# A query stage in two passes by tokens, and sixteen more prompt tokens that fetch their own expert rows

## The chip, the cores and the metric

The kernel runs on one core of one Trainium2 chip. The metric is the device time of one launch in microseconds (us). The kernel before took 1719.96 us, the median of three runs (1716.91 to 1726.47). A core has five engines with a queue of instructions each, which they work off in order: TensorE (PE; its weight loads are shown as PEld), VectorE (DVE), ScalarE (ACT), GpSimd (POOL) and SyncE (SP), which here only issues DMAs. POOL also issues the gathering DMAs. [...]

## The reference, cut to what matters

One layer over 512 prompt tokens and 128 sample tokens (8 sequences of 16), width 1024. The first half is a mixer (linear recurrence and sliding-window attention), and the change doesn't touch it. The second half, which takes most of the time, is a product-key expert layer:

```python
def peer(xn, w_query, sub_keys1, sub_keys2, expert_u, expert_v):
    q = (xn @ w_query).reshape(T, 8, 2, 128)                 # 8 heads, two halves
    s1 = einsum('thd,kd->thk', q[:, :, 0], sub_keys1)        # 128 keys a half
    s2 = einsum('thd,kd->thk', q[:, :, 1], sub_keys2)
    v1, i1 = top_k(s1, 16); v2, i2 = top_k(s2, 16)
    cand_s = v1[..., :, None] + v2[..., None, :]             # 256 pairs, of which 16 stay
    top_s, top_pos = top_k(cand_s, 16)
    idx = take_along_axis(i1 * 128 + i2, top_pos)            # 16 of 16384 experts
    gates = softmax(top_s)
    act = gelu(einsum('thkd,td->thk', expert_u[idx], xn))
    return einsum('thk,thkd->td', gates * act, expert_v[idx])
y = h + peer(rmsnorm(h))
```

So each token picks, in each of 8 heads, 16 experts out of 16384, and an expert is one row of `expert_u` and one of `expert_v` (1024 floats, 4 KB each).

## The kernel before, in words

Tokens lie in five tiles of 128: tiles 0 to 3 are the prompt, tile 4 is the samples. There are two ways to the expert layer. The first 448 prompt tokens (`SD`) go the *dense* way: all 16384 experts are multiplied with all 448 tokens, and a gate matrix that is zero nearly everywhere weighs the results. The 128 sample tokens and the last 64 prompt tokens (`HD`) go the *own* way: their expert rows are fetched one by one with gathering DMAs of 128 rows (one row to a partition).

Every fp32 matmul is done as three: an operand is split into a high part (rounded, by ACT) and a low part (the rest, by a subtraction), and high*high, high*low and low*high are added up. A weight *slab* of 1 MB is loaded by SP (`raw`), `high` (L93) makes `wh` on ACT, and `low` (L98, the work stands at L100) makes `wl` on the engine that it is given, POOL or DVE. `raw`, `wh` and `wl` have two buffers each.

The stages after the mixer, in order of the program:

1. *Query stage* (L840 to L966). The normed tokens are turned to columns by `turn_rows` (`xh`, `xl`). Eight slabs of `w_query` give 16 units `u` (head and half): a unit multiplies 128 query columns with all 640 tokens (`query_half`, then `proj_T`, two matmuls of 320 columns to each of 24 steps). `query_keys(u - 2)` then multiplies the finished queries of the unit two before with the 128 keys (five small matmuls, L914), copies the scores with ACT (L916), and finds the 16 best of each token on DVE (L919 to L924). In every second unit `next_slab(G)` splits the next slab, the low part on POOL.
2. *U stage* (loop at L1285, 64 iterations `c`). Each takes a slab of `expert_u` with 256 experts: 48 matmuls of 448 columns (`u_block`, L960), a gelu on ACT (L1280), and the result goes to DRAM (`Ad`). Beside it, DVE works through the *pieces*: `select(t)` joins the two halves' best to 16 experts with gates, and `matrix(t)` builds the gate matrix from one-hot pieces (L1122, L1126), which PE multiplies (L1134). `plan` deals the pieces out over the iterations by an estimated cost (`piece(2.4, ...)` is 2.4 us), evenly up to iteration `NS - 6`.
3. *V stage* (loop at L1339, 64 iterations). Each takes a slab of `expert_v`: `weigh` multiplies the activations with the gates on DVE (L1266), `weigh_split` splits them on ACT (L1271) and DVE (L1273), and 48 matmuls of 448 columns (L1359) add up.

The own way runs beside stages 2 and 3: `own_work(c)` first consumes on DVE the rows that have come (a dot product with the token at L1181, or a weighted addition at L1186) and then lets POOL fetch the next (L1174), three or four per iteration, 384 in all (192 of `u`, 192 of `v`), into a ring of six buffers. The work starts when `select(4)` is done.

Nothing reorders the program: each engine runs its instructions in the order in which the code writes them.

## Time and profile before

| | before |
|---|---|
| median of three runs | 1719.96 us |
| the profiled execution | 1711.95 us, its span 1710.2 us |
| PE / DVE / ACT / POOL busy | 98% / 83% / 40% / 40% of the span |
| bytes moved | 492.67 MB, mean 288 GB/s |
| chain that ended last | PE 75%, DVE 14%, DMA 5%, ACT 3%, issue 2% |

The times of instructions are those of the profiled execution, counted from the start of its span. A busy PE is not a PE at its peak, since matmuls overlap: a matmul of 448 columns is shown as 366 ns long while the next starts after about 202 ns. So the pace is read from starts, or from how many stand in a stretch. [...]

### The profile page before, as it was taken

What the parts mean: (1) busy time and instruction counts of PE and PEld (TensorE: products, weight loads), DVE (VectorE), ACT (ScalarE), POOL (GpSimd) and SP (SyncE); (2) the same over time, 40 slices, a digit from 0 to 9 for tenths busy, and PEclk for the clock granted to TensorE, in tenths of its full rate; (3) what the DMA queues carried; (4) which work ended last, traced back from release to release, by engine and by line L of the source; (5) the groups of instructions that cost most, each with busy time, mean ns of one, the idle gap of its engine ahead of it and who ended that gap; (6) DMA issues with size and microseconds to landing.
All of it is one profiled execution on the core that took longest, in us unless ns stands there. A gap on an engine that the chain in (4) does not pass through costs nothing.

```text
span 1710.2 us, 24851 instructions
## 1 busy us (share of the span) xinstructions
PE 1679.2 (98%) x9654; PEld 1546.7 (90%) x9654; DVE 1417.1 (83%) x2348; ACT 679.6 (40%) x790; POOL 690.2 (40%) x485
## 2 busy tenths in 40 slices
PE   8999999999999999999999999899999999999998
PEld 8887889999989898999899999899998999999998
DVE  7766465999789999899988885788887888888886
ACT  5457332233444544554455553322232232232322
POOL 4122003233134344444444433455454555455551
PEclk9999899999999999999999999999999999999999
DMA  5313233223689898999999999999999999999995
GB/s 169 104 48 113 76 105 90 75 70 126 249 277 322 308 377 291 370 389 348 314 379 344 372 352 403 397 380 368 384 374 335 405 376 385 375 377 376 369 350 201
DMA packets 180983, 492.67 MB, mean 288 GB/s; under 512 B 16817, under 2 KB 75057, under 8 KB 170225
## 3 DMA queue, kind: packets, MB, share of 16 engines
q1 hardware_dynamic: 124848, 288.68, 46.7%
q0 software_dynamic: 55296, 201.35, 31.4%
q8 instruction: 75, 1.23, 0.3%
q10 hardware_dynamic: 720, 1.05, 0.2%
q14 instruction: 44, 0.35, 0.1%
HBM read 426.11 MB, written 65.48 MB: 287 GB/s over the span
## 4 chain that ended last, share of the span: by engine, by line
PE 75%; DVE 14%; DMA 5%; ACT 3%; issue 2%; POOL 0%; DVEq 0%; ACTq 0%; SPq 0%
PE po L1359 35%; PE pa L960 21%; PE pa L113 7%; PE pb L1134 3%; DVE wl L100 2%; DMA gt<-Gd 2%; PE pb L638 2%; PE pa L638 2%; DVE ring L1181 2%; DVE h_rows L1181 2%; DMA raw<-in_u 2%; PE pb L914 1%; PE pa L857 1%; ACT wh L95 1%; DMA Gd<-stage 1%
## 5 line engine op out<-in xcount | busy, mean ns | idle before, releaser
L1359 PE MATMUL po<-ph,wh 128*128 128x448 f32 x1024 | 374.7, 366 | 3.5 <-ACT act L1280 1.9
L1359 PE MATMUL po<-pl,wh 128*128 128x448 f32 x1024 | 374.9, 366 | 3.2 <-DVE pl L1273 3.2
L100 DVE TENSOR_TENSOR wl<-raw,wh 128x2048 fp32r<-128x2048 f32 x135 | 308.8, 2288 | 83.5 <-ACT wh L95 82.8
L960 PE MATMUL pa<-xh,wh 128*128 128x448 f32 x1024 | 377.5, 369 | 0.0
L1359 PE MATMUL po<-ph,wl 128*128 128x448 f32 x1024 | 374.5, 366 | 0.0
L960 PE MATMUL pa<-xh,wl 128*128 128x448 f32 x1024 | 374.2, 365 | 0.2 <-DVE wl L100 0.2
L960 PE MATMUL pa<-xl,wh 128*128 128x448 f32 x1024 | 374.1, 365 | 0.0
L95 ACT ACTIVATE wh<-raw 128x2048 fp32r<-128x2048 f32 x146 | 279.5, 1914 | 226.9 <-PE po L1359 173.8
L1174 POOL DMA_INDIRECT h_rows<-in_u_rows,rowi x96 | 138.5, 1443 | 219.9 <-DVE h_rows L1181 164.1
L1174 POOL DMA_INDIRECT ring<-in_u_rows,rowi x96 | 136.8, 1425 | 194.3 <-DVE ring L1181 173.4
L1174 POOL DMA_INDIRECT h_rows<-in_v,rowi x96 | 155.9, 1624 | 143.4 <-DVE h_rows L1186 121.3
L1359 PEld LDWEIGHTS po<-ph,wh 128*128 128x128 f32 x1024 | 192.7, 188 | 19.5 <-ACT act L1280 2.2
L1359 PEld LDWEIGHTS po<-pl,wh 128*128 128x128 f32 x1024 | 192.7, 188 | 19.0 <-DVE pl L1273 3.8
L960 PEld LDWEIGHTS pa<-xh,wl 128*128 128x128 f32 x1024 | 192.3, 188 | 16.1 <-DVE wl L100 0.6
L1359 PEld LDWEIGHTS po<-ph,wl 128*128 128x128 f32 x1024 | 192.7, 188 | 15.3
L960 PEld LDWEIGHTS pa<-xh,wh 128*128 128x128 f32 x1024 | 192.4, 188 | 15.2 <-ACT act L1280 0.3
L960 PEld LDWEIGHTS pa<-xl,wh 128*128 128x128 f32 x1024 | 192.5, 188 | 15.1
L1174 POOL DMA_INDIRECT ring<-in_v,rowi x96 | 149.8, 1560 | 133.2 <-DVE h_rows L1186 109.2
L1280 ACT ACTIVATE act<-pa 128x448 f32<-128x448 f32 x128 | 71.5, 559 | 232.4 <-PE pa L960 225.1
L1271 ACT ACTIVATE ph<-at 128x896 fp32r<-128x896 f32 x64 | 61.0, 953 | 254.0 <-DVE at L1266 254.0
L1142 ACT ACTIVATE stage<-pb 128x512 f32<-128x512 f32 x112 | 109.8, 1129 | 89.9 <-PE pb L1134 89.9
L1273 DVE TENSOR_TENSOR pl<-at,ph 128x896 fp32r<-128x896 f32 x64 | 69.9, 1093 | 72.7 <-ACT ph L1271 72.7
(280 smaller groups left out, 2498.7 us busy)
## 6 DMA issues: line engine op xcount, KB each, us to landing
raw<-in_u SPq DMA_DIRECT2D x64, 1024.0 KB
raw<-in_v SPq DMA_DIRECT2D x64, 1024.0 KB
Ad<-act SPq DMA_DIRECT2D x64, 448.0 KB
Gd<-stage SPq DMA_DIRECT2D x28, 1024.0 KB
gt<-Gd SPq DMA_DIRECT2D x64, 448.0 KB
at<-Ad SPq DMA_DIRECT2D x64, 448.0 KB
raw<-in_w_query SPq DMA_DIRECT2D x8, 1024.0 KB
raw<-in_w_out SPq DMA_DIRECT2D x4, 1024.0 KB
```

Source lines behind the costliest of these rows:

```text
L95: A.activation(wh, raw, AF.Copy)
L100: eng.tensor_sub(wl, raw, wh.bitcast(F32))
L113: PE.matmul(ps[:, hf, :H2], a[:, k, cs], b[:, k, hf * H2:(hf + 1) * H2], start=(k == 0 and n == 0), stop=(k == KD - 1 and n == 2))
L638: PE.matmul(ps, a[:, k0 + k, ts_], b[:, k, :], start=(k == 0 and n == 0), stop=(k == CT - 1 and n == 2))
L960: PE.matmul(u_ps[c, n][:, :SD], a[:, k, n * P:(n + 1) * P], b[:, k, :SD], start=(k == 0 and m == 0), stop=(k == KD - 1 and m == 2))
L1142: A.activation(d["stage"][:, :, t0:t0 + 4].rearrange("p j t -> p t j"), d[n, f], AF.Copy, scale=1.0 / GSC)
L1174: G.indirect_dma_start(out=rows[n], out_offset=None, in_=table, in_offset=bass.IndirectOffsetOnAxis(ap=rowi[:, c:c + 1], axis=0))
L1181: V.scalar_tensor_tensor(row, row, 1.0, xrow[:, n // NS_], op0=ALU.mult, op1=ALU.mult, accum_out=dots[:, n:n + 1])
L1271: A.activation(ph, a2, AF.Copy)
L1273: V.tensor_sub(pl, a2, ph.bitcast(F32))
L1280: A.activation(act[c][:, n], u_ps[c, n][:, :SD], AF.Gelu_apprx_tanh)
L1359: PE.matmul(po[k][:, :SD], a[:, j, k * P:(k + 1) * P], b[:, j, :], start=(c == 0 and j == 0 and n == 0), stop=(c == NS - 1 and j == 1 and ...
```

## The change

The prompt tokens on the own way become 80: the last 64 as before, and 16 more (rows 48 to 63 of tile 3, `NC`). The dense width `SD` falls from 448 to 432. For these 16 tokens the rows are laid out with one head to a group of 16 partitions, so that their 2048 rows fill 16 more fetches of 128; a fetch round is now 208 rows of `u` and 208 of `v` (`NR`). Their outputs are summed over the 8 groups through DRAM at the end (`Yc`).

The query stage is written in two passes. The first multiplies all eight slabs with the own tiles 3 and 4 (256 columns), the second loads and splits the eight slabs again and multiplies them with tiles 0 to 2 (384 columns). In the second pass DVE works on `select(4)` and on the search of the dense tiles, as far as a budget of 4.2 us to a unit goes; the searches that are left are pieces of the U stage. Fetching starts in the second pass, one row per unit. The scores of the dense tiles wait in the `stage` buffers.

```diff
-SD = S - HD
+NC = 16
+C0 = P - HD - NC
+SD = S - HD - NC
-        + [i["w_out"][n] for n in range(4)] + [i["w_query"][n] for n in range(PH)]
+        + [i["w_out"][n] for n in range(4)] + [i["w_query"][n] for _ in range(2) for n in range(PH)]
...
+    def queries(ps, w, n, cols):
+        wh, wl = w
         for k in range(KD):
             for m, (a, b) in enumerate(((wh, xh), (wh, xl), (wl, xh))):
+                PE.matmul(ps[:, :cols.stop - cols.start], a[:, k, n * P:(n + 1) * P], b[:, k, cols],
                           start=(k == 0 and m == 0), stop=(k == KD - 1 and m == 2))
...
+    turn_rows(ND - 1)
+    turn_rows(ND)
+    scaled(turns[-1])
     for n in range(2):
-        query_half(n, 1)
+        queries(two[n], kc(slabs[A0 + 2]), n, OWN)
+        turn_rows(n)
+    turn_rows(2)
...
+    next_slab(G)
+    for u in range(2):
+        query_out(u, two[u], OWN)
+    for u in range(2, 2 * PH):
+        ps = wide()[:, 0]
+        queries(ps, kc(slabs[Q0 + u // 2]), u % 2, OWN)
+        own_keys(u - 2)
+        if u % 2 == 0:
+            next_slab(G)
+        query_out(u, ps, OWN)
...
+    for u in range(2 * PH):
+        ps = wide()[:, 0]
+        queries(ps, kc(slabs[Q0 + PH + c]), n, DENSE)
+        if u < 2:
+            own_keys(2 * PH - 2 + u)
+        else:
+            scores(u - 2 + 2 * PH, 3, later(u - 2))
+        for f in acts:
+            f()
+        if n == 0:
+            if c + 1 < PH:
+                next_slab(G)
+            else:
+                put(U, 0, G)
+                u_load(1)
+        query_out(u + 2 * PH, ps, DENSE)
+        used = max(used, 0.0) - 4.2
+        while used < 0:
...
+        if not todo:
+            own_step(n_pre, n_pre + 1)
+            n_pre += 1
...
+            if c == NR - 1:
+                nc.sync.dma_start(Yc.rearrange("h (t q) d -> (h t) (q d)", t=NC), y)
+                parts = p2.tile([P, PH, P], F32, name="parts", tag="y2")
+                nc.sync.dma_start(parts, Yc.rearrange("h r d -> r h d"))
+                rest = p2.tile([P, 2, P], F32, name="rest")
+                nc.sync.dma_start(rest[:, 0], Hd[ND - 1, C0:HD].rearrange("t (q d) -> (t q) d", d=P))
+                V.tensor_reduce(rest[:, 1], parts.rearrange("p h d -> p d h"), axis=AX.X, op=ALU.add)
+                V.tensor_add(rest[:, 0], rest[:, 0], rest[:, 1])
...
+                for dst, src in ((slots, ts), (rowi, ti)):
+                    nc.sync.dma_start(dst[0:HD, NS_:NB_], src[up, :HD])
+                    for h in range(PH):
+                        nc.sync.dma_start(dst[h * NC:(h + 1) * NC, NB_:], src[C0:HD, h * TK:(h + 1) * TK])
```

ACT in the query stage, two units of before: the score copies are L916, the split of the next slab L95, the copy of the unit's queries L905.

```order
L916 ACTIVATE s<-pb 128x512
L916 ACTIVATE s<-pb 128x128
L95 ACTIVATE wh<-raw 128x2048
L905 ACTIVATE q<-pa 128x640
L916 ACTIVATE s<-pb 128x512
L916 ACTIVATE s<-pb 128x128
L905 ACTIVATE q<-pa 128x640
```

The split of the next slab comes once in two units, behind the score copies. The same two units in the first pass of the changed kernel; L940 is the score copy, L97 the split, L932 the query copy.

```order
L940 ACTIVATE act<-pb 128x256
L97 ACTIVATE wh<-raw 128x2048
L932 ACTIVATE act<-pa 128x256
L940 ACTIVATE act<-pb 128x256
L932 ACTIVATE act<-pa 128x256
```

The split still stands behind the score copy of the unit that uses the slab before; what lies between two splits is now 256 columns wide, and later 384, where it was 640.

POOL from the query stage to the first fetches, before: the low parts of slabs are L100, the fetches L1174.

```order
L100 TENSOR_TENSOR wl<-raw,wh 128x2048 x9
L970 IOTA first_of 128x16
L970 IOTA first_of 128x48
L970 IOTA first_of 128x64
L970 IOTA first_of 128x128
L973 IOTA column 128x256
L976 IOTA io_4064 128x256
L100 TENSOR_TENSOR wl<-raw,wh 128x2048 x2
L1174 DMA h_rows<-in_u_rows,rowi 128x1024 x3
```

All low parts but two of `u` come ahead of the first fetch. In the changed kernel they are L102 and L1185:

```order
L970 IOTA io_2581 128x256
L102 TENSOR_TENSOR wl<-raw,wh 128x2048 x12
L1185 DMA h_rows<-in_u_rows,rowi 128x1024 x2
L102 TENSOR_TENSOR wl<-raw,wh 128x2048
L1185 DMA h_rows<-in_u_rows,rowi 128x1024
L1185 DMA ring_2561<-in_u_rows,rowi 128x1024
L102 TENSOR_TENSOR wl<-raw,wh 128x2048
```

POOL makes 19 low parts in place of 11, and the fetches of the second pass stand between the last of them.

DVE in the V stage of before, where the two halves of the 64 tokens' output are joined (L1190 waits for a DMA that has moved one half across partitions):

```order
L1273 TENSOR_TENSOR pl<-at,ph 128x896
L1186 SCALAR_TENSOR_TENSOR h_rows<-h_rows,slots 128x1024
L1186 SCALAR_TENSOR_TENSOR h_rows<-ring_2608,slots,h_rows 128x1024
L1190 TENSOR_TENSOR h_rows<-h_rows,y_11803 64x1024
L1186 SCALAR_TENSOR_TENSOR h_rows<-ring_2608,slots,h_rows 128x1024 x2
L100 TENSOR_TENSOR wl<-raw,wh 128x2048
```

One such wait stands in DVE's queue. The changed kernel has the like of it (L1206), and five iterations later this, where the eight groups' outputs are summed (L1215 needs the two DMAs through `Yc`):

```order
L1358 TENSOR_TENSOR pl<-at,ph 128x864
L1202 SCALAR_TENSOR_TENSOR yc<-ring_2561,slots,yc 128x1024
L1215 TENSOR_REDUCE rest<-parts 128x128
L1216 TENSOR_TENSOR rest<-rest 128x128
L1202 SCALAR_TENSOR_TENSOR h_rows<-h_rows,slots 128x1024 x2
L102 TENSOR_TENSOR wl<-raw,wh 128x2048
```

A second wait has come into DVE's row of the V stage, ahead of two rows and of the next slab's low part.

## Rows read from the trace of the kernel before

**Rows 1.** Busy by stage (query, U, V): stretch, PE, PEld, DVE, ACT, POOL, clock, DMA, GB/s.
```profile
260.00:383.00 123.00, 122.47 (x869) 122.24 (x870) 98.15 (x524) 35.11 (x54) 37.04 (x8) 1.00 0.24 73
383.00:1069.00 686.00, 681.09 (x3992) 626.69 (x3991) 606.79 (x1126) 326.86 (x342) 278.02 (x192) 1.00 0.91 327
1069.00:1700.00 631.00, 624.26 (x3076) 577.26 (x3075) 535.28 (x417) 185.85 (x135) 319.22 (x201) 1.00 0.96 366
```
**Rows 2.** Chain that ended last: start, length, what; matmuls of 256, 512, 320, 128 columns.
```profile
99.95 2.92 PE pb L186 x24
...
223.44 2.72 PE pa L638 x12
...
349.58 7.03 PE pa L113 x48
...
357.73 7.03 PE pa L113 x48
...
689.44 1.85 PE pb L1134 x32
```
**Rows 3.** The V stage's matmuls of 448 columns in one stretch, columns as in the first group.
```profile
1330.00:1690.00 360.00, 360.00 (x1778) 333.60 (x1777) 1.00 0.97 370
```
**Rows 4.** One line's view, L960: duration in ns, first and last start of its matmuls.
```profile
L960 PE MATMUL pa<-xh,wh x1024: 362/365/472, 383.0 to 1068.6; 128*128 128x448 f32 x171
```
**Rows 5.** Timeline of ACT at a slab change of the query stage: start, length, what.
```profile
276.07 0.77 ACT L916 ACTIVATE s<-pb 128x512 f32<-128x512 f32 x2 [7.23 <-PE pb L914]
276.72 1.92 ACT L95 ACTIVATE wh<-raw 128x2048 fp32r<-128x2048 f32 x1
```
**Rows 6.** Timeline of POOL at the same slab change.
```profile
278.71 4.63 POOL L100 TENSOR_TENSOR wl<-raw,wh 128x2048 fp32r<-128x2048 f32 x1 [11.53 <-ACT wh L95]
```
**Rows 7.** One tile's view, the keys: duration in ns, first and last start of the score matmuls.
```profile
L914 PE MATMUL pb<-sk,q x160: 270/275/275, 275.0 to 389.0; 128*128 128x128 f32 x160
```
**Rows 8.** Timeline of PE at the query stage's first transposes.
```profile
247.76 1.91 PE L836 MATMUL pb<-ident,xn 128*128 128x128 f32 x16
```
**Rows 9.** Groups by line, ACT: busy us, then mean ns of one.
```profile
L1048 ACT ACTIVATE ix<-it 128x2048 f16<-128x2048 f16 x10 | 18.5, 1895 | 0.0
```
**Rows 10.** PE's busy time and granted clock (then DMA, GB/s) after two gaps.
```profile
1074.00:1075.00 1.00, 0.71 (x2) 0.50 0.85 313
...
1077.00:1078.00 1.00, 1.00 (x5) 0.83 1.04 420
...
1318.00:1321.00 3.00, 1.32 (x6) 1.00 0.99 324
```
**Rows 11.** Timeline of DVE in the query stage: the first step of two tiles' searches.
```profile
278.29 0.28 DVE L919 MAX8 val<-s 128x8 f32<-128x128 f32 x1
279.86 0.28 DVE L919 MAX8 val<-s 128x8 f32<-128x128 f32 x1
```
**Rows 12.** Chain of waits in the U stage: DVE's rows and one-hot pieces.
```profile
512.13 3.43 DVE h_rows L1181 x6
...
590.40 1.15 DVE oh L1122
...
592.80 1.15 DVE oh L1122
```
**Rows 13.** Timeline of DVE, one iteration of the V stage, from low part to low part.
```profile
1402.42 2.28 DVE L100 TENSOR_TENSOR wl<-raw,wh 128x2048 fp32r<-128x2048 f32 x1
...
1406.87 1.09 DVE L1273 TENSOR_TENSOR pl<-at,ph 128x896 fp32r<-128x896 f32 x1 [1.16 <-ACT ph L1271]
...
1409.19 2.61 DVE L1186 SCALAR_TENSOR_TENSOR h_rows<-h_rows,slots 128x1024 f32<-128x1024 f32 x2
1411.71 2.28 DVE L100 TENSOR_TENSOR wl<-raw,wh 128x2048 fp32r<-128x2048 f32 x1
```
**Rows 14.** Timeline of DVE where the 64 tokens' halves are joined.
```profile
1312.39 1.22 DVE L1190 TENSOR_TENSOR h_rows<-h_rows,y 64x1024 f32<-64x1024 f32 x1 [3.00 <-DMA y<-h_rows]
```
**Rows 15.** Timeline of SP's queue at the same place: the issue of that DMA.
```profile
1309.41 0.47 SPq L1189 DMA_DIRECT2D y<-h_rows  x1
```

More of the change, by code (lines that the diff above doesn't have):

```diff
@@ L817, in hybrid_layer @@
     Xd = dram.tile([P, D], F32, name="Xd")
-    X3 = dram.tile([HD, D], F32, name="X3")
+    X3 = dram.tile([NC + HD, D], F32, name="X3")
+    Yc = dram.tile([PH, P, P], F32, name="Yc")
     ssq = wk.tile([P, NT], F32, name="ssq")
@@ L933, in put @@
         table[c][2] = low(table[c][0], table[c][1], eng)
-    Q0 = A0 + 2
-    next_slab(G)
-    query_out(0, two[0])
-    query_out(1, two[1])
-    for u in range(2, 2 * PH):
-        c, n = u // 2, u % 2
-        if n == 0 and c + 1 == PH:
-            u_load(0)
-        ps = wide()
-        proj_T(ps, kc(slabs[Q0 + c]), xh, xl, n)
-        query_keys(u - 2)
-        if n == 0:
-            if c + 1 < PH:
-                next_slab(G)
-            else:
-                put(U, 0, G)
-                u_load(1)
-        query_out(u, ps)
     u_ps = {}
@@ L1149, in matrix, with later, rest_of_plan @@
             piece(2.4, lambda n=n: hot(n), pe=lambda n=n: place(n), act=lambda n=n: store(n))
-    for t in (ND, ND - 1):
-        select(t)
-    n_own = len(pieces)
-    select(0)
-    matrix(ND - 1)
-    select(1)
-    matrix(0)
-    select(2)
-    matrix(1)
-    matrix(2)
+    select(ND)
+    own_first = pieces[:]
+    del pieces[:]
+    held, held_s = [], {}
+    def later(u):
+        if u == 2 * PH - 1:
+            held_s[u] = qs[u + 2 * PH][:, 3 * P:6 * P]
+        else:
+            if u % 5 == 0:
+                held.append(tb.tile([P, NK, TG], F32, name="stage", tag="stage", bufs=3)
+                            .rearrange("p a b -> p (a b)"))
+            held_s[u] = held[u // 5][:, u % 5 * 3 * P:(u % 5 + 1) * 3 * P]
+        return held_s[u]
+    def rest_of_plan():
+        select(ND - 1)
+        select(0)
+        matrix(ND - 1)
+        select(1)
+        matrix(0)
+        select(2)
+        matrix(1)
+        matrix(2)
     NO = 2 * NR
-    NS_ = PH * TK
     rows = {}
@@ L1198, in hybrid_layer, with own_step @@
     NS = NK // 2
[L1201 to L1229 removed]
+    n_pre = 0
+    def own_step(n0, n1):
         for n in sorted(rows):
@@ L1235, in own_work, with own_keys @@
             fetch(n)
+    def own_work(c):
+        own_step(*[n_pre + min(NO - n_pre, (NO - n_pre) * x // (2 * NS - 2)) for x in (c, c + 1)])
+    Q0 = A0 + 2
+    own_tiles, tiles = (ND - 1, ND), tuple(range(ND - 1))
+    def own_keys(u):
+        s = qs[u][:, 2 * P:4 * P]
+        scores(u, 2, s)
+        search(u, own_tiles, s)
+    next_slab(G)
[8 more added lines that the diff above has]
+        query_out(u, ps, OWN)
@@ new lines, in hybrid_layer @@
+    todo, acts, sought, used = list(own_first), [], 0, 0.0
+    for u in range(2 * PH):
+        c, n = u // 2, u % 2
+        if n == 0 and c + 1 == PH:
+            u_load(0)
+        ps = wide()[:, 0]
[6 more added lines that the diff above has]
+            f()
+        acts = []
+        if n == 0:
+            if c + 1 < PH:
+                next_slab(G)
+            else:
+                put(U, 0, G)
+                u_load(1)
+        query_out(u + 2 * PH, ps, DENSE)
+        if u < 1:
+            continue
+        used = max(used, 0.0) - 4.2
+        while used < 0:
+            if todo:
+                p = todo.pop(0)
+                p[2]()
+                used += p[0]
+                if p[4]:
+                    acts.append(p[4])
+                if p[5]:
+                    break
+            elif sought < u - 2:
+                search(sought, tiles, held_s[sought])
+                sought += 1
+                used += 5.0
+            else:
+                break
+        if not todo:
+            own_step(n_pre, n_pre + 1)
+            n_pre += 1
@@ new lines, in hybrid_layer @@
+    put(U, 1, G)
+    scores(4 * PH - 2, 3, later(2 * PH - 2))
+    u_block(0, 0)
+    scores(4 * PH - 1, 3, later(2 * PH - 1))
+    for u in (2 * PH - 1, *range(sought, 2 * PH - 1)):
+        piece(5.0, lambda u=u: search(u, tiles, held_s[u]))
+    rest_of_plan()
+    plan = [[] for _ in range(NS + 4)]
+    total = sum(p[0] for p in pieces)
+    used, c = 0.0, 0
+    for p in pieces:
+        while used >= total * (c + 1) / (NS - 6):
+            c += 1
+        plan[c].append(p)
+        used += p[0]
+        if p[5]:
+            c += 1
@@ L1253, in group_piece @@
         gt, at = ga[g]
-        n = NCH // 4
-        nc.sync.dma_start(gt[:, q * n:(q + 1) * n], Gd[g][:, q * n:(q + 1) * n])
+        part = slice(q * NCH // 4, (q + 1) * NCH // 4)
+        nc.sync.dma_start(gt[:, part], Gd[g][:, part])
         nc.sync.dma_start(at[:, 2 * q:2 * q + 2], Ad[g][:, 2 * q:2 * q + 2, :])
```

137 lines of the change are left out of this document (54 added, 83 removed).

## The prediction

> **What bounds the kernel now.** I read the table by stage first [rows 1]: PE is busy in 122.5 of 123 us of the query stage, 681 of 686 of the U stage and 624 of 631 of the V stage, with the clock at 1.00. DVE is next: 606.8 of 686 in U, 535.3 of 631 in V. POOL and ACT are far from full anywhere. Then the chain, for PE's pace. A matmul's own length (365 ns at 448 columns [rows 4]) is no pace, since the next one starts sooner; counts are. The chain gives 24 matmuls of 256 columns in 2.92 us, 48 of 320 in 7.03, 12 of 512 in 2.72 [rows 2], so 121.7, 146.5 and 226.7 ns each; a stretch of V gives 1778 of 448 columns in 360 us, 202.5 ns [rows 3]. [...] So U and V are bound by columns: 3072 matmuls each, 622 us, plus in U 56 one-hot pieces at 0.93 us (two take 1.85 [rows 2]), 52 us, and some 3 us of transposes: 677 of 686 [rows 4]. The rest, about 9 us in U and 6 in V, is PE waiting.
>
> Third, the timelines of the query stage, since the change rewrites it. A unit lasts 8.15 us there [rows 2], 7.03 of queries and 1.11 of five score matmuls (0.22 us each). The reader is to see one chain at a slab change: scores start at 275.0 [rows 7], ACT copies them at 276.07, splits the next slab from 276.72 [rows 5], POOL makes its low part from 278.71, for 4.63 us, to 283.34 [rows 6]. That slab is wanted by the unit after next, about 284.5. So the chain of 8.3 us from the end of a unit's queries is hidden by one unit of 8.15 us and the scores ahead of it, with 1 us to spare. It costs nothing now, and it is nearly as long as what covers it.
>
> **The change part by part.** *Narrower matmuls.* 16 columns at 0.417 ns are 6.7 ns, over 6144 matmuls 41 us: 20.5 in U and as much in V. Two one-hot pieces fall away: 1.9 us. The width of 432 is not in the trace; 512 and 320 columns lie 13.3 ns above their columns' time and 448 lies 15.8, so 432 may come out 4.2 to 9.3 ns cheaper (26 to 57 us). I take the middle.
>
> [...]
>
> *Query stage, work.* It now has 16 units of 24 matmuls at 256 columns (121.7 ns) and 16 at 384 (between 146.5 and 202.5: 174.5): 46.7 + 67.0 = 113.7 us, against 16 x 48 x 146.5 = 112.5. Scores up to the U stage: 77 against 70 small matmuls, 1.6 us. The first queries need the tiles turned last, whose mean square comes ahead of all turns on ACT: 0 to 3, I take 1. Together +3.8 us. Before, the stage ran from 247.8 [rows 8] to 383.0 [rows 4].
>
> *Query stage, the split.* This is the term that decides. ACT's and POOL's rows show that the split still stands behind the score copy of the unit before, but a unit is now half as long. In the first pass, counted from the end of an even unit's queries: two scores before the copy in place of four take 0.44 off, one copy of about 0.33 for 0.77 the like, so the low part is ready at 8.34 - 0.76 = 7.6 us. PE meanwhile has two scores, one unit and two scores (0.44 + 2.92 + 0.44) and the two matmuls that need only `wh`, 4.05 us. It waits 3.6 us, seven times (six slabs of the pass and the first of the second): 25.2 us. In the second pass the low part is ready at 7.9, PE has 0.67 + 4.19 + 0.67 + 0.35 = 5.9: 2.05 us, seven times: 14.4; for the first slab of `u` 1.3. The very first of these slabs has no queries at all to hide it: ACT's split follows the last turn, so PE waits about 0.7 + 2.0 + 4.63 = 7.3 us, of which before hid all behind three half units. And once ACT's exponent and two spreads (0.3 + 2 x 1.9 us [rows 9]) stand ahead of a split: 4.1. Sum 52.3 us. From both sides: nothing, if ACT and POOL could run ahead, which the order excludes; 80, if every slab lost its full 7.6.
>
> *The clock.* After the gap of some 5 us between the last U matmuls [rows 4] and 1074.3, the granted clock stood at 0.50 up to about 1077.3; after the gap of 1.7 us before 1321 it stayed at 1.00 [rows 10]. [...] I count one for the 7.3 us wait: +2. The 3.6 us waits lie between; they are a rival below.
>
> *U stage.* DVE changes places with PE in part of it. In place of `select(4)` and 15 tiles' searches, it has six units of search left over (3 tiles at 1.57 us [rows 11]) and some 23 more rows (1.15 us [rows 12]). In iterations 3 to 17 no one-hot piece stretches PE's time: PE needs 15 x 9.41 = 141 us, DVE 15 low parts at 2.29, 48 rows (55), 12 searched tiles (19) and two selections: 157. For a selection I take 24 us: of DVE's 606.8 us in U, 61 low parts, 177 rows, 56 one-hot pieces and 15 searched tiles leave 105 us for five of them, 21 each without their short gaps. Of the 16 us, 7 are taken up by the low part being made an iteration ahead, 9 are PE's wait. The second selection adds 2; SP's 18 small DMAs for slots and rows, in one go at 0.47 us each [rows 15], hold the next slab load up for 8: I take 5, between nothing and 8. With one-hot pieces DVE needs 2.4 us for each [rows 12] and PE gives 0.93: there PE is last again. So some 16 to 17 us of waits for 8.5: U gains 20.5 + 1.9 - 8 = 14.4 us.
>
> *V stage.* DVE's iteration with three rows is 9.29 us long [rows 13], its 1.16 us wait for ACT's `ph` included; a fourth row makes 10.6. With 432 columns it loses 0.1. 49 iterations of three and 14 of four take 597 us; PE takes 64 x 9.41 = 602. So DVE has no slack left, and each hold-up passes to PE. The first is as before, 3.0 + 1.2 us [rows 14], for a DMA issued at 1309.4 [rows 15]. The second is new: two DMAs one behind the other, each at least as long as that one, and a reduction over a strided view of 128x1024 (1.1 to 2.2 us, by the 1.1 to 1.3 of the two-operand forms), 8 to 20 us; I take 8.3. Behind it wait two rows and the next low part, and so PE. V gains 20.5 - 9.5 = 11 us.
>
> *DMA.* 8 MB of slabs and 16 MB of rows are added in stretches at 73 to 370 GB/s, where single microseconds go to 420 [rows 1, 10]: nothing, while they arrive a slab ahead.
>
> Sum: 3.8 + 52.3 + 2 - 14.4 - 11 = +32.7. The profiled execution took 1711.95 us (span 1710.2), so 1744.6 by its clock; the median of the runs is 8 above it, and the same difference on the median of 1719.96 gives 1753.
>
> **The rivals.** *The clock falls in the first pass.* For: 3.6 us gaps are nearer to the 5 us gap than to 1.7. Against: each is followed by 6.7 us of dense work. Eight times 1.7 us more: 1766. [...]
>
> *DVE takes U and V whole.* For: it is 16 us over in the stretch above and level in V. Against: the one-hot iterations, two thirds of U, leave it free. If nothing of the 41 us comes back: 1778.
>
> *432 columns are paced like 320 and 512,* at 193.3 ns: 2.5 ns more, 15 us at most, DVE permitting: 1738.
>
> *The split stays hidden (the other side).* Place: ACT's row at a slab change. If ACT and POOL got a slab's parts ready within 4 us of the unit's end in the first pass and 5.9 in the second, the waits of 25.2 + 14.4 + 1.3 go and the sum is -8: 1711; with the widest saving per column 1700. It decides as soon as more than 33 of the 52 us are hidden. For it: ACT is under a third busy there [rows 1]. Against: its order, and POOL's 4.63 us, which alone is more than 4.
>
> **How the numbers follow.** What I forecast 0.55, with its own range of 1738 to 1766; clock 0.14, DVE 0.13, pace 0.10, hidden split 0.08. Half a per cent of 1720, 8.6 us, is about what can be told from no change, so faster is under 1711 and slower over 1729. The hidden split is half faster and half the same; the pace rival and the low end of the forecast add a little to the same; all else is slower: 0.06, 0.07, 0.87. The range of 1728 to 1778 leaves out the hidden split and the worst of DVE and clock.
>
> **What would show it.** In the profile after, the first U matmul should start some 56 us later than 383.0; PE's groups of queries should wait for POOL's `wl`, about 3.6 us in each second unit of 256 columns and 2 in those of 384; PE's busy share of the stage should fall to some 70%. 448's 202.5 ns should become about 195.8. V should show a DVE wait of 6 us or more at the reduction, with PE idle behind it. I am wrong if PE doesn't wait for `wl` in the query stage, or if U and V together come back by more than 35 us or less than 10.

## The result and the profile after

The changed kernel took 1787.07 us, the median of four runs (1779.88 to 1790.43), the kernel before 1721.49 beside it: a ratio of 1.0375 (95% interval 1.033 to 1.042), slower by some 65 us. The forecast was 1753, in a range of 1728 to 1778. The profiled executions lie 78.5 us apart in span (1788.7 against 1710.2): the profile after is of the slowest of its runs, that of before of an execution (1711.95 us) faster than all the runs beside it. So 13 of the 78.5 us are the choice of executions. The steps below are accounted for in these spans.

| | before | after | difference |
|---|---|---|---|
| up to the first U matmul | 383.0 | 462.2 | +79.2 |
| U stage, to the first V matmul | 688.3 | 695.2 | +6.9 |
| V stage, to the end | 638.9 | 631.3 | -7.6 |

The forecast had +58, -14.4 and -11. The windows by stage of the changed kernel (columns as in [rows 1]; the query stage in its two passes):

```profile
268.00:346.00 78.00, 53.49 (x365) 52.08 (x365) 36.41 (x192) 19.76 (x33) 32.19 (x8) 0.85 0.32 108
346.00:462.00 116.00, 95.74 (x510) 93.00 (x510) 82.67 (x355) 34.26 (x47) 49.07 (x17) 0.87 0.31 109
462.00:1157.00 695.00, 670.13 (x3958) 635.27 (x3957) 626.32 (x1166) 315.74 (x335) 311.39 (x213) 0.98 0.95 340
1157.00:1788.00 631.00, 610.61 (x3104) 583.46 (x3104) 533.85 (x406) 183.68 (x135) 309.96 (x200) 0.99 0.96 366
```

Against [rows 1], PE's busy share in the first pass falls from nearly all to 69%, and the granted clock from 1.00 to 0.85. In U PE is idle for 25 us where it was for 5. What PE waited for, from 249 us on, by the view of waits, the five largest (us in total, times, longest):

```profile
PE pa L866 <- POOL wl L102: 42.2, 15, 4.0
PE po L1444 <- ACT ph L1356: 11.8, 2, 7.7
PE pb L1131 <- DVE ow L1123: 10.9, 6, 4.8
PE pa L958 <- DVE wl L102: 5.0, 4, 2.1
PE pa L866 <- ACT act L932: 4.6, 2, 2.9
```

The first line is the wait for the split that was forecast, 15 times. The timeline at one slab change answers to [rows 5, 6] (ACT: score copy and split; POOL: low part; PE: the matmuls that need it):

```profile
278.51 0.38 ACT L940 ACTIVATE act<-pb 128x256 f32<-128x256 f32 x1 [9.44 <-PE pb L939]
278.79 1.91 ACT L97 ACTIVATE wh<-raw 128x2048 fp32r<-128x2048 f32 x1
...
280.77 4.52 POOL L102 TENSOR_TENSOR wl<-raw,wh 128x2048 fp32r<-128x2048 f32 x1 [7.67 <-ACT wh L97]
...
281.74 0.28 PE L866 MATMUL pa<-xl,wh 128*128 128x256 f32 x1
285.34 0.58 PE L866 MATMUL pa<-xh,wl 128*128 128x256 f32 x1 [3.33 <-POOL wl L102]
285.73 0.42 PE L866 MATMUL pa<-xh,wh 128*128 128x256 f32 x1
285.94 0.42 PE L866 MATMUL pa<-xl,wh 128*128 128x256 f32 x1
...
309.85 0.39 PE L866 MATMUL pa<-xh,wl 128*128 128x256 f32 x1 [3.32 <-POOL wl L102]
310.07 0.28 PE L866 MATMUL pa<-xh,wh 128*128 128x256 f32 x1
310.19 0.28 PE L866 MATMUL pa<-xl,wh 128*128 128x256 f32 x1
...
320.07 0.39 PE L866 MATMUL pa<-xh,wl 128*128 128x256 f32 x1 [3.33 <-POOL wl L102]
...
410.31 0.44 PE L866 MATMUL pa<-xh,wl 128*128 128x384 f32 x1 [1.81 <-POOL wl L102]
...
411.38 0.52 PE L866 MATMUL pa<-xh,wh 128*128 128x384 f32 x1
411.70 0.52 PE L866 MATMUL pa<-xl,wh 128*128 128x384 f32 x1
...
418.73 0.33 PE L866 MATMUL pa<-xl,wh 128*128 128x384 f32 x1
418.90 0.34 PE L866 MATMUL pa<-xh,wl 128*128 128x384 f32 x1
```

The split stands behind the score copy and PE waits 3.33 us: that is the forecast. What it did not have is the pace behind the wait. Starts are 0.21 us apart at 285.73 and 0.12 at 310.07 for the same 256 columns, 0.32 at 411.38 and 0.17 at 418.73 for 384: half speed (the granted clock is 0.50 from 285.3 to 288.5, 1.00 from 310 to 314). Starts slower than 1.3 times the full pace come in 13 such stretches of 3 to 6.4 us, one behind nearly every wait, also behind those of 1.8 us in the second pass; against the full pace each loses 1.5 to 2.7 us, 25 us in sum. Three waits of 3.3 us (309.85, 320.07, 330.28) are followed by full pace, and from the first to the second of them the same work takes 10.2 us where from 285.34 to 298.14 it took 12.8. So the wait's length alone doesn't decide. Three runs below (three, four and seventeen) leave this stage as it is: in them and this one, half speed follows all 24 waits for `wl` of 1.8 to 2.2 us and all four of 4.0, but only 17 of the 32 of 3.1 to 3.8, and the first U matmul comes at 455.3 to 465.7. What decides is open.

In U two stops behind SP's small DMAs stand out (first SP's issues, then DVE and PE behind them):

```profile
599.71 5.24 SPq L1088 DMA_DIRECT2D slots<-ts  x8
...
605.63 5.02 SPq L1088 DMA_DIRECT2D rowi<-ti  x8
610.75 1.23 SPq L92 DMA_DIRECT2D raw<-in_u  x1
...
619.31 2.29 DVE L102 TENSOR_TENSOR wl<-raw,wh 128x2048 fp32r<-128x2048 f32 x1 [7.73 <-ACT wh L97]
...
1087.60 4.62 SPq L893 DMA_DIRECT2D xrow<-X  x8
...
1097.68 1.23 DVE L1192 SCALAR_TENSOR_TENSOR h_rows<-h_rows,xrow 128x1024 f32<-128x1024 f32 x1 [10.11 <-DMA xrow<-X]
...
1101.36 1.89 PE L1131 MATMUL pb<-ow,oh 128*128 128x128 f16 x16 [4.79 <-DVE ow L1123]
```

The eighteen DMAs for slots and rows take 11.5 us of SP's queue, and the next slab's load stands behind them. The eight that refill `xrow` can start only when DVE has used its old rows, and DVE then needs them at once: 10.1 us of DVE, 4.8 of PE. The forecast did not have this second stop at all.

### The profile page after: what moved, and what is told of

Same layout as the page of the kernel before. It is cut to its first block, busy times and chain, and to the rows that moved or that the text cites. A ratio compares the mean times of both kernels' runs of the same rounds, so it can differ in the third digit from the quotient of the medians.

```text
span 1788.7 us, 25007 instructions
## 1 busy us (share of the span) xinstructions
PE 1678.9 (94%) x9622; PEld 1582.4 (88%) x9622; DVE 1453.2 (81%) x2397; ACT 685.8 (38%) x808; POOL 760.5 (43%) x525
## 4 chain that ended last, share of the span: by engine, by line
PE 37%; DVE 37%; issue 8%; DMA 8%; ACT 5%; POOL 4%; SPq 1%; ACTq 0%; DVEq 0%; POOLq 0%
PE pa L958 14%; DVE wl L102 11%; DVE h_rows L1202 7%; PE po L1444 6%; PE pa L866 6%; DVE ring L1192 3%; DVE h_rows L1192 3%; POOL wl L102 3%; DMA raw<-in_v 3%; DVE at L1351 3%; ACT ph L1356 2%; PE pa L115 2%; PE pb L1131 2%; DMA raw<-in_u 2%; PE pa L640 2%
## 5 line engine op out<-in xcount | busy, mean ns | idle before, releaser
L1444 PE MATMUL po<-ph,wh 128*128 128x432 f32 x1024 | 368.4, 360 | 12.5 <-ACT ph L1356 11.8
L958 PE MATMUL pa<-xh,wl 128*128 128x432 f32 x1024 | 371.3, 363 | 6.3 <-DVE wl L102 5.0
L958 PE MATMUL pa<-xh,wh 128*128 128x432 f32 x1024 | 374.1, 365 | 2.9 <-ACT act L1365 2.9
L1444 PE MATMUL po<-pl,wh 128*128 128x432 f32 x1024 | 368.9, 360 | 4.1 <-DVE pl L1358 4.1
L958 PE MATMUL pa<-xl,wh 128*128 128x432 f32 x1024 | 370.6, 362 | 0.0
L1444 PE MATMUL po<-ph,wl 128*128 128x432 f32 x1024 | 367.7, 359 | 0.0
L102 DVE TENSOR_TENSOR wl<-raw,wh 128x2048 fp32r<-128x2048 f32 x135 | 308.5, 2285 | 58.3 <-ACT wh L97 58.0
L97 ACT ACTIVATE wh<-raw 128x2048 fp32r<-128x2048 f32 x154 | 294.7, 1914 | 159.4 <-PE po L1444 108.0
L1185 POOL DMA_INDIRECT h_rows<-in_v,rowi x104 | 161.8, 1556 | 160.9 <-DVE h_rows L1202 120.9
L1185 POOL DMA_INDIRECT ring<-in_u_rows,rowi x103 | 148.0, 1437 | 185.9 <-DVE ring L1192 162.7
L1185 POOL DMA_INDIRECT ring<-in_v,rowi x104 | 159.2, 1531 | 154.2 <-DVE h_rows L1202 115.9
L1185 POOL DMA_INDIRECT h_rows<-in_u_rows,rowi x105 | 145.9, 1390 | 181.6 <-DVE h_rows L1192 159.4
L1356 ACT ACTIVATE ph<-at 128x864 fp32r<-128x864 f32 x64 | 59.3, 926 | 323.6 <-DVE at L1351 317.2
L1365 ACT ACTIVATE act<-pa 128x432 f32<-128x432 f32 x128 | 69.3, 542 | 242.5 <-PE pa L958 240.0
L1192 DVE SCALAR_TENSOR_TENSOR h_rows<-h_rows,xrow 128x1024 f32<-128x1024 f32 x105 | 127.5, 1245 | 20.2 <-DMA xrow<-X 10.1
## 6 DMA issues: line engine op xcount, KB each, us to landing
at<-Ad SPq DMA_DIRECT2D x64, 432.0 KB, 10.9
```

The lines of the kernel that those rows point to most:

```text
L97: A.activation(wh, raw, AF.Copy)
L102: eng.tensor_sub(wl, raw, wh.bitcast(F32))
L958: PE.matmul(u_ps[c, n][:, :SD], a[:, k, n * P:(n + 1) * P], b[:, k, :SD], start=(k == 0 and m == 0), stop=(k == KD - 1 and m == 2))
L1185: G.indirect_dma_start(out=rows[n], out_offset=None, in_=table, in_offset=bass.IndirectOffsetOnAxis(ap=rowi[:, c:c + 1], axis=0))
L1192: V.scalar_tensor_tensor(row, row, 1.0, xrow[:, n // NS_], op0=ALU.mult, op1=ALU.mult, accum_out=dots[:, n:n + 1])
L1356: A.activation(ph, a2, AF.Copy)
```

## Experiments

All times are medians of four or more runs, ratios are to the kernel before, run beside them.

**One (e1), the split written first.** In the first pass, and in the second likewise:

```diff
         queries(ps, kc(slabs[Q0 + u // 2]), u % 2, OWN)
-        own_keys(u - 2)
         if u % 2 == 0:
             next_slab(G)
+        own_keys(u - 2)
```

> The split of the next slab is written ahead of the score copies in both passes of the query stage, so that ACT starts it when the first unit of a slab starts and not when that unit's scores are done; nothing is left out. Theory A (the waits for the split cost their own length, and the clock that falls behind each of them as much again): PE's waits for POOL's wl in the query stage fall from 42 us to under 10, the half-clock time behind them from about 30 us lost to under 8, the first U matmul comes at about 400 and not at 462, and the time falls by some 60 us, to 1725. Rival B (the half clock there has another cause than these waits): the waits go, the clock stays near 0.86, the first U matmul comes at about 430, 1755. Rival C (ACT and POOL cannot run ahead, because slabs arrive too late): no change, 1787.

1751.36 us, ratio 1.0191 (1.014 to 1.0241). PE's waits in the query stage from 268 us on:

```profile
PE pa L866 <- ACT act L932: 8.3, 2, 5.4
PE pa L866 <- POOL wl L102: 4.9, 4, 3.8
```

42 us of waits for `wl` became 4.9 while those for `act` grew from 4.6 to 8.3; the 13 slow stretches became three (7.7 us lost, at the begin of the stage and of the second pass), and the first U matmul came at 412.0, 50 us earlier: 34 us fewer waits and 17 us less half clock. So theory A holds for the stage, though its 400 was not reached. Its time was not reached at all (1751 for 1725, near the 1755 of rival B): only 34 us of span were left, because U took 710.8 us in place of 695.2.

**Two (e2), the waits filled.** The waits stay, PE works through them:

```diff
             for m, (a, b) in enumerate(((wh, xh), (wh, xl), (wl, xh))):
+                for _ in range(fill if k == 0 and m == 2 else 0):
+                    PE.matmul(pas[-1][:, 1, :256], wh[:, 0, :P], xh[:, 0, OWN], start=True, stop=True)
...
+        queries(ps, kc(slabs[Q0 + u // 2]), u % 2, OWN, 0 if u % 2 else 16 if u == 2 else 26)
```

> The waits stay, but PE is kept busy in them: behind the two matmuls that need only wh, each first unit of a slab has 26 more matmuls of 256 columns in the first pass (3.1 us, the wait is 3.3) and 14 in the second (1.7, the wait is 1.8), into a PSUM bank that nothing reads; nothing is left out. Theory A (idle time lets the clock fall): the granted clock between 269 and the first U matmul goes from 0.86 to over 0.96, each unit runs at the full pace, and the first U matmul comes some 25 us earlier, about 437: 1762. Rival B (the clock falls for another reason): clock and time stay, 1787, or grow with the added matmuls. Were the filling too long for the waits, the time would grow by the part that is over, at most 10 us.

1782.56 us, ratio 1.0354 (1.029 to 1.0417). The two passes by windows, as above:

```profile
268.00:346.00 78.00, 73.89 (x590) 72.27 (x589) 42.52 (x224) 21.81 (x35) 35.35 (x8) 0.98 0.31 102
346.00:441.00 95.00, 89.33 (x556) 87.72 (x555) 73.79 (x288) 30.95 (x41) 42.84 (x16) 0.98 0.36 133
```

The clock is 0.98 in place of 0.85 and 0.87, and the first U matmul comes at 443.2, 19 us earlier, with the splits as late as ever (in the first pass POOL makes a low part every 10.3 us; the full-pace waits above lie 10.2 apart). Against the 455.3 to 465.7 of the runs with the stage left as it was, that is 12 to 22 us from the clock alone. The time doesn't show it (the interval overlaps that of the changed kernel), since U took 10 us of it back (705.6) and V 3 (634.3).

**Three (e3), the own way's DMAs.** The eighteen small DMAs are kept in a list, `moves`, and issued two to an iteration, and the 16 tokens' columns go into the half of `xrow` that is free after row 127:

```diff
-            if n == NB_ - 1:
+            if n == NS_ - 1:
                 rows_by_head()
...
+        for _ in range(2):
+            if moves:
+                nc.sync.dma_start(*moves.pop(0))
```

> The own way's small DMAs leave the path: the 18 for slots and row numbers are issued two to an iteration and not in one go, and the 16 tokens' columns go into the half of xrow that is free after row 127, so that their 8 DMAs are issued 64 rows ahead of their use; nothing is left out. Theory A (these two holds cost what PE shows behind them): DVE's waits of 7.7 us at 619 and 10.1 us at 1097 go, and with them PE's 3.8 and 4.8 us and about 4.7 us of half clock: 13 us less, 1774. Rival D (DVE is the bound there and the time moves into later waits for DVE): within 4 us of 1787. Small DMAs spread over iterations could also hold slab loads up one by one: then DVE shows waits of 1 us in each of 9 iterations.

1772.22 us, ratio 1.0333 (1.0273 to 1.0394), an interval that by itself still touches the changed kernel's. The trace tells it: both DVE waits are gone (the longest left in U is 4.6 us), and U is 679.7 us in place of 695.2, the 13 us of theory A and a little more.

**Four (e4), the sum over groups later** (the reduction written two iterations behind its DMAs).

```diff
-                V.tensor_reduce(rest[:, 1], parts.rearrange("p h d -> p d h"), axis=AX.X, op=ALU.add)
+                joins.append((parts, rest))
...
+        if joins and c == joins_at[-1] + 2:
+            parts, rest = joins.pop()
+            V.tensor_reduce(rest[:, 1], parts.rearrange("p h d -> p d h"), axis=AX.X, op=ALU.add)
```

> In the V stage the sum over the eight groups is written two iterations behind its two DMAs, in place of directly behind them; nothing is left out. Theory A (the new wait costs its length and a half-clock stretch): DVE's wait of 7.7 us at 1400 goes, PE's 7.7 us wait behind it and 2.6 us of half clock go: 10 us less, 1777. Rival D (DVE is level with PE in V, so that what is freed is lost behind it): DVE's wait goes, but PE waits for pl or ph in later iterations, 1784 to 1787.

1786.42 us, ratio 1.038 (1.0319 to 1.044): no change that the times show. DVE's 7.7 us wait is gone and PE's 7.7 us wait for `ph` with it (11.8 us in all became 6.0), V is 4.7 us shorter in the trace (626.6); the rest of the 10 us did not come. This experiment is inconclusive.

**Five (e5), the three edits in one.**

> The three edits in one: split ahead of the score copies, small DMAs spread and xrow refilled early, the sum over the groups two iterations late; nothing is left out. Alone they gave -36, -15 and -1 us. If they add up: 1735. Theory DVE-bound (in e1 the U stage grew by 16 us as the query stage shrank by 50, because DVE's work there did not shrink): the U stage still shows DVE busy in over 94% of its first 260 us and PE waiting for wl and ow, 15 to 20 us with the clock's part, and the time ends at 1730 to 1740, over the kernel before. Rival (the 16 us came from the two DMA holds alone): with these gone U falls to about 675 us or less and the time to 1718.

1735.11 us, ratio 1.0079 (1.005 to 1.0108): they add up, and the kernel before is still faster, by 0.8%. U stays at 691 us, 12 more than in three. A likely reason stands where POOL makes a low part while DVE has rows to do (POOL first, then DVE):

```profile
392.38 4.59 POOL L102 TENSOR_TENSOR wl<-raw,wh 128x2048 fp32r<-128x2048 f32 x1 [1.95 <-ACT wh L97]
...
393.01 5.04 DVE L1193 SCALAR_TENSOR_TENSOR h_rows<-h_rows,xrow 128x1024 f32<-128x1024 f32 x1
...
397.99 1.21 DVE L1193 SCALAR_TENSOR_TENSOR ring<-ring,xrow 128x1024 f32<-128x1024 f32 x1
```

A row of 1.21 us takes 5.04 and ends 1.1 us behind POOL's subtraction, about its own length. Such stretched instructions, summed over DVE's timeline from 250 to 470 us, cost 25 us here and 7 in the changed kernel. They cost 25 in one and 20 in two as well, the runs whose U grew by 16 and 10 us, and 8 in three, whose U did not.

**Six (e6), low parts moved from DVE to POOL in U** (as five, and):

```diff
-            put(*((U, c + 1) if c + 1 < NS else (Pv, 0)), G if c <= 2 else V)
+            put(*((U, c + 1) if c + 1 < NS else (Pv, 0)), G if c <= 2 or c in range(4, 20, 2) else V)
```

> As e5_all, and eight of the low parts of u (every second one from iteration 4 to 18) are made by POOL and not by DVE: DVE has 8 x 2.29 = 18 us less to do in the stretch in which it is full; nothing is left out. Theory DVE-bound: the U stage falls by 10 to 18 us against e5_all, PE's waits for DVE's wl nearly vanish before iteration 20: 1718 to 1725. Rival (PE waits for single hold-ups, not for DVE's amount of work): as e5_all, within 4 us. Rival POOL (its low part of 4.6 us and three fetches of 1.5 us fill an iteration of 9.4 us): PE waits for POOL's wl, or DVE for rows, and it is slower than e5_all by 5 to 15 us.

1738.55 us, ratio 1.0107 (1.0057 to 1.0157): nothing gained. DVE got rid of 18 us of work, and its stretched instructions grew from 25 to 47 us between 250 and 650. The relief was paid back by the same hold.

**Eleven (e11), the low parts of the second pass moved from POOL to DVE** (as five, with those of the first four slabs of `u`, which are not shown):

```diff
-                next_slab(G)
+                next_slab(V)
```

> As e5_all, with the low parts of the second pass and of the first slabs of u (11 in all) made by DVE in 2.29 us each, and not by POOL; nothing is left out. Theory lock (a DVE instruction with two operands in SBUF that comes while POOL makes its low part waits until POOL is done: in e5_all rows of 1.21 us take up to 5.04, 21 us in sum): no row of DVE takes over 1.5 us, DVE has 25 us more to do and 21 less to wait, and the time is that of e5_all within 6 us, 1729 to 1741. Rival (POOL's work doesn't hold DVE, the long rows have another cause): DVE's 25 us come on top in a stretch in which it is full, 1750 to 1760.

1731.91 us, ratio 1.0068 (1.0045 to 1.0091): DVE makes eleven more low parts in 2.28 us each at no cost in the time, and its rows up to 470 us are all short (mean ns, the number behind the comma):

```profile
L1193 DVE SCALAR_TENSOR_TENSOR h_rows<-h_rows,xrow 128x1024 f32<-128x1024 f32 x12 | 14.4, 1213 | 0.0
L1193 DVE SCALAR_TENSOR_TENSOR ring<-ring,xrow 128x1024 f32<-128x1024 f32 x10 | 12.0, 1216 | 0.0
```

In five the same groups have means of 2045 and 2142 ns. So POOL's subtraction holds DVE's rows. What the holds alone cost in time this run doesn't tell, since it puts 25 us of DVE's work in the place of 25 us of holds, and U stays (688.3).

**Seven (e7), the width alone** (in the kernel before; the 16 tokens' expert outputs are left out):

```diff
-SD = S - HD
+SD = S - HD - 16
```

> The kernel before with one number changed: the dense width 432, nothing done for the 16 tokens that fall out (their expert outputs are left out), so queries, searches, rows and DMAs stay as before. Theory A (PE is the bound in U and V, a column costs 0.42 ns): 6.8 ns x 6144 matmuls and two one-hot pieces go: 1718 - 44 = 1674, V's stretch of matmuls 602 us in place of 622. Theory DVE-bound (DVE, 89% busy in U and level with PE in V, takes a part back): U comes back by less than 15 us, or V shows PE waiting for pl: 1685 to 1700.

1680.54 us, ratio 0.9753 (0.9704 to 0.9803): -43 us. Matmuls in a stretch of V, here and then in the changed kernel:

```profile
1330.00:1650.00 320.00, 317.65 (x1623) 1.00 0.99 377
```

```profile
1415.00:1735.00 320.00, 318.86 (x1629) 1.00 1.00 383
```

317.65 / 1623 and 318.86 / 1629 are both 195.7 ns, against 202.5 at 448 columns [rows 3]. The forecast had 195.8 and 43 us (41 and 1.9); the time agrees to a microsecond, closer than its interval, some 8 us either way, can tell.

**Eight (e8), the two passes alone** (in the changed kernel; the tokens' rows, DMAs and sum are gone with it, not shown):

```diff
-NC = 16
+NC = 0
```

> The changed kernel with no tokens of the second kind (the number of them set to 0): two passes in the query stage, dense width 448, 192 rows of u and of v as before, no sum over groups; nothing is left out of the result. Theory A (the two passes cost 79 us up to the first U matmul, and the narrower matmuls gain 42 us in U and V of which the tokens' rows, DMAs and the left-over searches take all back): the first U matmul again at about 462, U and V at 202.5 ns a matmul together no longer than in the changed kernel plus 10 us: 1787 to 1800. Rival (the tokens' own work is what costs, and the two passes much less): under 1770.

1792.68 us, ratio 1.0424 (1.0371 to 1.0477). The two passes cost some 70 us, the width gives 43 back, so the tokens' own work costs some 35 to 40 of the 65 us that both halves make.

**Nine and ten (e9, e10), the other half alone**: one pass as before, with the sixteen tokens and the width 432; in ten with the edits of three and four. Nine to the kernel before, at its core:

```diff
-SD = S - HD
+NC = 16
+C0 = P - HD - NC
+SD = S - HD - NC
...
-    NR = PH * TK + HD
+    NB_ = PH * TK + HD
+    NR = NB_ + TK
```

> The other half of the change alone: the query stage of the kernel before, in one pass, with the sixteen tokens, their DMAs and the dense width 432 as in the changed kernel; nothing is left out. The two passes alone gave 1793, both halves 1787, so if the halves add up this one stands 6 us under the kernel before, 1715 to 1718: the 43 us of the width less some 37 us of the tokens' own rows, waits and DMAs. Theory two-passes (the searches left over for the U stage and POOL's splits beside DVE's rows are part of those 37 us, and go with the two passes): 1695 to 1708. Rival (the rows, denser since they begin later, fill DVE): 1718 to 1730.

> As e9_tokens_alone, with the small DMAs spread two to an iteration, xrow refilled 64 rows ahead, and the sum over groups two iterations late; nothing is left out. In the changed kernel these edits gave 16 us together: 16 us under e9_tokens_alone, so about 1701, and faster than both kernels. Rival (DVE is full there, so that the waits' time is lost behind them): 0 to 5 us under e9_tokens_alone.

1736.36 (ratio 1.0099, 1.0066 to 1.0132) and 1729.02 us (1.0043, 1.0021 to 1.0065). The halves don't add up: without the two passes the tokens' work costs about 60 us. Ten, expected at 1701 by what its edits gave in the changed kernel, is 7 us under nine. Rows begin later, 3.35 come to an iteration, and in ten's V PE waits 20.7 us for `pl` and 10.9 for `ph`, which ACT makes from what DVE weighs.

**Twelve, fourteen and sixteen (e12, e14, e16), V's order.** DVE waits 1.1 us for ACT's `ph` in each iteration of V. Twelve (on ten) puts the rows into that gap, fourteen (on ten) also puts the slab's split last, sixteen (on fourteen) also loads a group's gates in two iterations and joins the halves two iterations later. The edit of fourteen:

```diff
-            put(Pv, c + 1, V)
             weigh(c + 1)
+        own_work(NS + c)
+        if c + 1 < NS:
             weigh_split(c + 1)
-        own_work(NS + c)
+            put(Pv, c + 1, V)
```

> As e10_tokens_mended, and in the V stage the rows are added up between the weighing and the low part pl, so that DVE works on rows while ACT makes ph (it waited 1.1 us for that in each of 63 iterations, 70 us in sum); nothing is left out. Theory DVE-bound V (with 3.35 rows to an iteration DVE needs some 9.65 us, 1.1 of them the wait, where PE needs 9.39; PE waits 20.7 us for pl and 10.9 for ph in V): DVE's wait for ph goes, PE's waits for pl fall under 6 us, V from 657 to under 635 us: 1700 to 1709, faster than both kernels. Rival (pl, now behind three rows, comes too late for PE's second matmul of each iteration): PE waits for pl as before or longer, 1729 or slower.

> As e10_tokens_mended, and in the V stage an iteration is written weigh, rows, ph and pl, and only then the split of the next slab; nothing is left out. In e12 the rows stood between wl and pl, and the chain from the slab buffer that PE leaves free over wh 1.9, wl 2.3, the weighing 1.0, rows 4 to 5 and pl 1.0 came to 11 us, over PE's 9.4: it was 28 us slower. Theory chain (in each iteration of V DVE's work that waits for PE's buffers has to stand together and last): here rows and weighing wait for nothing that PE holds, the chain is ph 0.9, pl 1.0, wh 1.9, wl 2.3, some 5 us, and DVE's work of 8.5 us fits: PE's waits in V fall from 39 to under 10 us and the time to 1690 to 1702, faster than both kernels. Rival (DVE's amount of work in V is too much in any order): 1722 to 1735.

> As e14_low_last, with each group's gates and activations loaded in two iterations, two quarters each, in place of four (so that the last quarter is issued three iterations ahead of its use and not one), and the join of the two halves written two iterations behind its DMA; nothing is left out. Theory (in e14 DVE no longer waits for ph but, being ahead, for DMAs: 51.5 us for gt, 7.0 for at, 13.7 for y, and PE behind it 34 us for pl and wl): DVE's waits for DMAs in V fall under 20 us, PE's under 15, and the time by some 15 to 25 us, to 1700 to 1710, faster than both kernels. Rival (DVE's amount of work is the bound in V, 3.35 rows in 9.4 us): DVE's waits go, PE's for pl and wl stay over 25 us, 1720 to 1726.

Twelve: 1757.16 us, ratio 1.0225 (1.0184 to 1.0267), PE's waits for `pl` went from 20.7 to 60.9 us, and DVE's for the split `wh`, which needs a buffer that PE frees, from 9.4 to 103.4: the rows now stand in the chain from that buffer to `pl`. The same edit on five (e13) gave 1764.06, that of fourteen on five (e15) 1745.13 where 1717 to 1725 was expected. Fourteen: 1725.66, ratio 1.0037 (1.0013 to 1.0061): DVE, no longer behind ACT, now runs into DMAs, 51.5 us for `gt` (44.4 in e15). The time falls in the range of its rival (DVE's amount of work is too much in any order), but sixteen, with the same work, rules that out. Sixteen: 1693.72, ratio 0.9862 (0.9807 to 0.9918), 23 us faster than the kernel before, with nothing left out; its two edits were not tried apart, nor on the two passes. DVE's work in V is the same in all of them (552 to 557 us). PE's waits in V in ten, and in sixteen:

```profile
PE po L1398 <- DVE pl L1312: 20.7, 32, 2.3
PE po L1398 <- ACT ph L1310: 10.9, 3, 5.8
PE po L1398 <- ACT act L1319: 7.3, 1, 7.3
```

```profile
PE po L1403 <- DVE wl L102: 6.0, 5, 1.7
PE po L1403 <- ACT act L1324: 6.0, 1, 6.0
PE po L1403 <- DVE pl L1317: 2.3, 1, 2.3
```

**Seventeen (e17), no searches left for U** (18 searched tiles, by the expectation 28 us of DVE; their results are left out):

```diff
-        piece(5.0, lambda u=u: search(u, tiles, held_s[u]))
+        piece(5.0, lambda u=u: [V.memset(x[:, 0:ND - 1, u // 2, u % 2], 0) for x in (val, idx)])
```

> The changed kernel, in which the searches left over for the U stage are replaced by filling their places with zeros (18 searched tiles, 28 us of DVE; their results are left out). Theory DVE-bound (the first 120 us of U have DVE 96% busy, and its amount of work sets PE's waits and the half clock behind them there): PE's waits for DVE up to 680 us fall by 6 us or more, DVE's busy share there under 88%, and the time by 8 to 15 us: 1772 to 1779. Rival (single hold-ups: the eighteen small DMAs at 599 and the selection's own chain): PE's waits at 598 to 622 stay, and the time falls by under 5 us: 1782 to 1787.

1781.12 us, ratio 1.0369 (1.0311 to 1.0426). The first 120 us of U here, and in the changed kernel:

```profile
457.00:577.00 120.00, 119.89 (x615) 115.28 (x616) 91.63 (x209) 44.19 (x46) 73.63 (x47) 1.00 0.92 338
```

```profile
462.00:582.00 120.00, 116.90 (x590) 111.35 (x590) 113.01 (x363) 41.44 (x44) 70.01 (x45) 0.99 0.90 321
```

DVE falls from 94% to 76% there and PE no longer waits; U is 6.6 us shorter (688.6), and the time is between the two forecasts. But behind that stretch, at the DMAs and the selection, PE waits nearly as before (in U 20.6 us, against 24.4). So the amount of DVE's work is the smaller part of U's loss, single hold-ups the larger: neither theory alone.

## Why the prediction was wrong, step by step

| step | forecast | measured in the spans |
|---|---|---|
| narrower matmuls (U and V) | -41, pieces -1.9 | -42 (195.7 ns), pieces -1.9 |
| waits of the query stage, its start among them | 53 | 50: `wl` 42.2, `pa` 4.6, start 3 |
| the clock in the query stage | +2 | +25 |
| the rest of the stage (widths, scores, begin) | +3 | +5 |
| U: waits of PE above those of before | +8 | +20, and 10 at half clock |
| V: waits of PE above those of before | +9.5 | +10, and 2 at half clock above that of before |

*What bounds the kernel* and *narrower matmuls* held: columns at 0.42 ns, worth 43 us when nothing else changes (seven). No run shows as such the 0.417 ns a column that the forecast took: from 320 to 512 columns [rows 2] give 0.418, from 320 to 448 [rows 2, 3] 0.44, and seven, from 448 to 432, 0.42.

*The split* held. 3.6 us were said for the first pass and 3.3 came, 2.05 and 1.8 for the second. Experiment one moves the same work to another place and all but 4.9 us of the waits go.

*The clock* is the step that failed. It counted one half-speed stretch, on the ground that a gap of some 5 us had one behind it and a gap of 1.7 us none [rows 10], and left the waits of the split as a rival for the first pass alone. The reading was wrong already: what it took for one gap is two waits with a matmul between them, and both are shorter than the waits of 3.6 us that it forecast. Nor does a run show the 1.7 us that it took as lost in such a stretch: by [rows 10] the clock was 0.50 for some 3 us, half of which is 1.5, an estimate, and the stretches of the trace after lost 1.5 to 2.7 each.

```profile
1071.27 0.47 PE L1359 MATMUL po<-ph,wh 128*128 128x448 f32 x1 [1.85 <-ACT act L1280]
1074.29 0.74 PE L1359 MATMUL po<-pl,wh 128*128 128x448 f32 x1 [2.55 <-DVE pl L1273]
```

In the trace after, 13 half-speed stretches follow, in the second pass as well, and experiment two gives back 19 us by nothing but work in the gaps. With the stretches in U (10) and V (2 above before), half clock costs 37 us for the 2 forecast, 35 of the 46 us by which the span's sum was off. (The median was off by 34: 1787 for 1753.) So the likeliest case and the rival on the clock were one case: the waits that the first forecast bring the second. Between the waits of 1.8 to 4 us lie 7 to 12 us of work here; the trace shows half speed behind most of these waits and full speed behind three.

The clock alone doesn't carry the miss, though. Where it is mended in the query stage (two), the time is still 1782.56, since U lengthens when the stage ahead of it gets shorter, by 10 us there and by 16 in one. The sum had no such term. That the holds of DVE's rows by POOL (five) are its cause is likely by their size, but not shown apart.

*U stage* was said to gain 14.4 and lost 6.9. This is the second step that failed: the waits were mis-sized by 12 us. SP's burst was taken at 0.47 us a DMA from the one row there was [rows 15] and came at 0.64, 11.5 us in sum. The refill of `xrow` was not counted: its eight DMAs follow the last use of the old rows and precede the first of the new, a wait that the change adds in DVE's queue and that the code shows. Experiment three takes both away for 15 us. The 9 us for DVE's amount of work are of the size of what seventeen gives (6.6), which takes away more work than that term was for, so the agreement is loose.

*V stage* was near, -11 against -7.6: the reduction's wait is 7.7 us on DVE and on PE (8.3 said), with a stretch at clock 0.50 behind it:

```profile
1409.00:1414.00 5.00, 4.63 (x12) 0.50 1.01 398
```

*The rivals.* "DVE takes U and V whole" gave the right size: together they came back by 0.7 us, under the 10 that the prediction named as its limit. That is luck in part: its mechanism was only a piece of it, since U's DMA holds and half clock cost more than DVE's work, and in seven the columns came back whole. The pace rival and the hidden split are out; the split could have been hidden by moving one call in each pass, but the change as written didn't.

## What to carry to other kernels

Price a new wait on TensorE at its length and at the half-speed stretch behind it together, here 1.5 to 2.7 us for most waits of 1.8 to 4, and count them all: the repeated waits of 1.8 us cost clock every time (24 of 24), those of 3.3 us about half the time (17 of 32). Then ask what the next stage does when this one gets shorter: of 50 and 19 us won in the query stage (one and two), 34 and 6 were left in the span. Look at which engine waits before choosing a split's place: first in its iteration paid in the query stage (one), last in its iteration paid in V only once the loads came earlier (sixteen). When work is moved to an engine that is 90% busy, list each wait it brings into that queue (refills that stand between last and first use, bursts of small DMAs ahead of a slab load) before summing its busy time.

## What the runs showed of the hardware

While POOL subtracted (4.6 us, both operands in SBUF), DVE's instructions with two tensors as operands there ended only behind POOL: rows of 1.21 us took 2.3 to 5.0 (five), and a `cand` group 5.3 for 0.9, 0.1 us behind a subtraction of 4.7 (six). The searches' instructions beside it (MAX8, FIND_INDEX8 and MATCH_REPLACE8 of 128x128) kept their 0.28 to 0.30 (five), and with the low parts on DVE the rows up to 470 us had means of 1.21 and 1.22 (eleven).

Filling waits with matmuls whose result nobody reads kept the clock at 0.98, where it had been 0.85 to 0.87, and made the real work behind them faster: the first U matmul came at 443.2 in place of 462.2 (two). Small DMAs that each cover 16 partitions took SP 0.58 to 0.66 us apiece to issue; sixteen of them and two larger ones stood 11.5 us ahead of a slab load (the changed kernel).
